# A hybrid decoder block on one core: values' evacuations and two logits tiles placed ahead of the gated branch's transposes, filler weights loaded sooner, row sums turned at a head's third step

## The chip, the cores and the metric

The kernel runs on one core of a Trainium2 chip. The metric is the device time of one execution in microseconds (us), the median of three runs. The engines are TensorE (PE, with its weight loads listed apart as PEld), VectorE (DVE), ScalarE (ACT), GpSimd (POOL) and SyncE (SP), which issues most of the DMAs. Each engine works through its own instructions in order; between engines they wait for each other's semaphores.

## The reference

One decoder block over 1024 tokens, width 1024, float32 throughout: RMSNorm, one input projection, then two branches side by side, forgetting attention and chunked spatial gating; both go into one output projection with a residual. A gated MLP with a causal convolution and a last RMSNorm follow.

```python
xn = rmsnorm(h, norm_mix_g[layer])
proj = xn @ w_in[layer]
q, k, v = ...                       # 8 heads of 64 each
log_f = jax.nn.log_sigmoid(proj[..., G_END:] + b_forget[layer])
# attention, blocks of 128 queries
logits = jnp.einsum('bqhd,bkhd->bhqk', qi, k) * scale
logits = logits + ci[..., None] - c_k          # c = cumsum(log_f)
logits = jnp.where(causal, logits, -jnp.inf)
p = jax.nn.softmax(logits, axis=-1)
att = jnp.einsum('bhqk,bkhd->bqhd', p, v)
# spatial gating, chunks of 128 tokens, 8 groups of 64
mixed = jnp.einsum('gij,bnjgd->bnigd', w, vc) + b_s.T[None, None, :, :, None]
sg = u * mixed                                 # u, vg: gelu of their part of proj
h = h + jnp.concatenate([att, sg], axis=-1) @ w_out[layer]
h = h + conv_ffn(rmsnorm(h, norm_ffn_g[layer]), ...)
return rmsnorm(h, norm_final_g)
```

## The kernel before, in words

[...]

**Stages.** Input projection (gate values u and v, then attention values, then queries and keys), spatial gating, attention, output projection with residual and second norm, up-projection with convolution, down-projection. The values' product is finished last of the first stage; its last four tiles leave PSUM through `evac_v` (L655): a ScalarE copy scaled by the row's norm, and a VectorE instruction for the remainder. Both write V. Helpers hide their line: these instructions stand under L44 in the profile.

**Spatial gating.** `spatial` (L679) does 24 matmuls (L690 to L692), and for each of eight groups two VectorE instructions that write A (again under L44), the gated branch's result, in place of u. `turn_sg(hf)` (L698) transposes one half of it in four groups of four transposes (L705), each group into one bank; ScalarE casts the bank into G (L707) and VectorE subtracts for the remainder (L708). The output projection of the gated branch needs G.

**Attention.** Eight heads. `logits(h, j)` (L778) takes query block j of head h: GpSimd masks the diagonal block (L790), TensorE does two matmuls per 512 keys (L796, L797) into a PSUM tile of 1024 columns, VectorE adds the forgetting sums, clips and takes the minimum in one instruction (L798), and ScalarE exponentiates and adds up the row sums (L800). Blocks go from 7 (1024 keys) down to 0 (128 keys). `turn_p` (L802) transposes probabilities (L813), copies them to SBUF (L814) and takes the remainder (L815); `values` (L820) multiplies them with V (L832), two halves of 512 queries per head, and `L840`/`L841` move each half's product tile to H. A head is five steps (`STEPS`); in each, the next step's `turn_p` goes out before the present step's `values`, and the next head's logits come in between, the widest tile at step 0, the one with 896 keys at step 1, two at each later step (`NEXT`). Head 0's logits have no such cover and stand ahead of the loop.

**Row sums.** `row_tail(h)` (L733), at step 1 of head h: VectorE takes the reciprocal of the row sums (L738), TensorE turns them (L739), ScalarE copies them (L740) and writes them out to DRAM (L741), and SP reads them back as a broadcast over partitions into H (L742). For the last pair of heads `pair_half` multiplies them into the products on VectorE (L756), casts (L757) and subtracts (L758); for the other pairs GpSimd does this.

**Fillers.** `sg_out` (L845) is a generator: each step is one tile of the gated branch's output projection, twelve matmuls (L874 to L876), with a residual tile loaded (L870) and the result written to DRAM (L878). `fill(key)` takes as many steps as `FILLS` (L21) says; key (-1, j) is behind head 0's logits tile j, key (h, s) behind step s of head h. The first step loads and splits its weights (`wos`).

**Loads on SP.** `head_loads(h)` issues five loads for a head's queries, keys and forgetting sums, those of heads 0 and 1 ahead of the loop. `wo_load` (L887) loads the output projection's weights near the end, which GpSimd splits (L899, L900); the loads of the up-projection's first weights (`wup`, L977 and L995) follow on SP, and L742 of the last head behind them.

**PSUM.** Eight banks of 2 KB. Attention has a pool of its own ("psb"): two tiles of 4 KB with tag "L" for logits, four of 2 KB with tag "b" for everything else, fillers too. The tags get their addresses in the order of their first use in the program. The next stage has another pool ("psc") over the same banks, with four tiles of tag "b" and four of tag "s"; a tile there waits until whatever last used its bank has been read. The output projection (`wmm`, L1026 to L1028) takes its tiles from "b" and "s" in turn, the first four with k = 0, 1, 2 ahead of k = 3.

**Order.** A scheduler places each engine's instructions by priority in program order, and by edges that hold one instruction behind another (`after`, `seq`, `Line`); `seq` keeps TensorE's attention work in the order in which it is written.

## Time and profile before

| | us |
|---|---|
| median of three runs | 1076.2 (1076.04 to 1078.09) |
| profiled execution | 1076.44 |
| its span, first to last instruction | 1074.7 |
| TensorE busy | 1054.8 |
| VectorE busy | 892.9 |
| ScalarE busy | 571.0 |
| GpSimd busy | 237.2 |

How to read it: a row of the timeline has the start in us from the span's start, the busy time, the engine, the line and operation, the tile written and those read, shapes and, behind an x, the number of instructions put together in one row; in square brackets is the engine's idle time ahead of it and what released it. A row of waits has the engine with the tile and line that waited, what it waited for, the total in us, the number of waits and the longest. "SPq" and "ACTq" are DMA issues on these engines. Attention runs from about 223 to 387 us of the span.

### The profile page before, as it was taken

What the parts mean: (1) busy time and instruction counts of PE and PEld (TensorE: products, weight loads), DVE (VectorE), ACT (ScalarE), POOL (GpSimd) and SP (SyncE); (2) the same over time, 40 slices, a digit from 0 to 9 for tenths busy, and PEclk for the clock granted to TensorE, in tenths of its full rate; (3) what the DMA queues carried; (4) which work ended last, traced back from release to release, by engine and by line L of the source; (5) the groups of instructions that cost most, each with busy time, mean ns of one, the idle gap of its engine ahead of it and who ended that gap; (6) DMA issues with size and microseconds to landing.
All of it is one profiled execution on the core that took longest, in us unless ns stands there. A gap on an engine that the chain in (4) does not pass through costs nothing.

```text
span 1074.7 us, 14461 instructions
## 1 busy us (share of the span) xinstructions
PE 1054.8 (98%) x5013; PEld 875.8 (81%) x5013; DVE 892.9 (83%) x1303; ACT 571.0 (53%) x985; POOL 237.2 (22%) x219
## 2 busy tenths in 40 slices
PE   9999999989999899999999999999999999999997
PEld 6888788778888788878888888888888888888886
DVE  5985798777777869999899999989988776898774
ACT  6666644456666845764444444444444444454653
POOL 0002134020223651054333333333322000000000
PEclk9999999999999999999999999999999999999999
DMA  9242257957556335132244523223331899433442
GB/s 338 97 140 97 68 159 213 265 165 215 162 177 225 120 128 185 72 118 97 98 137 161 172 69 127 99 98 99 107 118 46 289 327 319 123 95 97 140 125 96
DMA packets 66297, 160.80 MB, mean 150 GB/s; under 512 B 7976, under 2 KB 8240, under 8 KB 66224
## 3 DMA queue, kind: packets, MB, share of 16 engines
q1 hardware_dynamic: 65792, 159.32, 45.5%
q8 instruction: 39, 0.64, 0.2%
q10 hardware_dynamic: 432, 0.57, 0.1%
q14 instruction: 34, 0.28, 0.1%
HBM read 117.06 MB, written 42.80 MB: 149 GB/s over the span
## 4 chain that ended last, share of the span: by engine, by line
PE 74%; DVE 2%; issue 2%; DMA 2%; ACT 2%; POOL 0%; DVEq 0%; ACTq 0%; POOLq 0%; SPq 0%
PE k L1369 19%; PE qa L1117 11%; PE qc L1117 11%; PE qd L1117 11%; PE qb L1117 5%; PE pb L832 2%; PE pb L813 2%; PE pf L874 1%; PE pf L876 1%; PE pf L875 1%; PE pl L796 1%; PE pl L797 1%; DMA raw<-wos 1%; PE pb L1026 1%; PE pb L1028 1%
## 5 line engine op out<-in xcount | busy, mean ns | idle before, releaser
L1369 PE MATMUL k<-whb,wha 128*128 128x512 f32 x924 | 209.7, 389 | 0.0
L1369 PEld LDWEIGHTS k<-whb,wha 128*128 128x128 f32 x924 | 173.3, 188 | 36.2 <-DVE wha L160 0.2
L1117 PE MATMUL qc<-xT,whb 128*128 128x512 f32 x540 | 129.8, 389 | 0.0
L1117 PE MATMUL qa<-xB,wha 128*128 128x512 f32 x528 | 127.2, 390 | 0.0
L1117 PEld LDWEIGHTS qc<-xT,whb 128*128 128x128 f32 x540 | 101.3, 188 | 21.2 <-ACT whb L154 0.2
L1117 PEld LDWEIGHTS qa<-xB,wha 128*128 128x128 f32 x528 | 98.8, 188 | 20.8 <-DVE wha L160 0.4
L154 ACT CAST wha<-sg 128x512 fp32r<-128x512 f32 x77 | 47.7, 622 | 96.9 <-PE k L1369 86.6
L154 ACT CAST whb<-sg 128x512 fp32r<-128x512 f32 x82 | 50.6, 618 | 85.8 <-PE qc L1117 68.5
L160 DVE TENSOR_TENSOR wha<-sg,wha 128x512 fp32r<-128x512 f32 x77 | 52.8, 688 | 41.0 <-ACT wha L154 40.9
L1117 PE MATMUL qd<-xB,whb 128*128 128x512 f32 x264 | 63.8, 389 | 0.5 <-DVE h L1236 0.5
L1117 PE MATMUL qd<-xT,whb 128*128 128x512 f32 x264 | 63.6, 389 | 0.0
L815 DVE TENSOR_TENSOR pt<-pb,pt 128x512 fp32r<-128x512 f32 (+1 forms) x80 | 50.0, 635 | 14.5 <-ACT pt L814 13.4
L160 DVE TENSOR_TENSOR whb<-sg,whb 128x512 fp32r<-128x512 f32 x82 | 58.3, 711 | 4.4 <-ACT whb L154 4.3
L1117 PE MATMUL qb<-xT,whb 128*128 128x512 f32 x252 | 60.8, 389 | 0.0
L1004 POOL TENSOR_TENSOR sg<-raw 128x512 f32<-128x512 f32 x20 | 30.9, 1546 | 134.2 <-DVE whb L160 76.0
L1117 PEld LDWEIGHTS qd<-xB,whb 128*128 128x128 f32 x264 | 49.5, 188 | 11.2 <-issue 0.9
L1117 PEld LDWEIGHTS qd<-xT,whb 128*128 128x128 f32 x264 | 49.5, 188 | 10.3
L1117 PEld LDWEIGHTS qb<-xT,whb 128*128 128x128 f32 x252 | 47.3, 188 | 9.8
L814 ACT CAST pt<-pb 128x512 fp32r<-128x512 f32 (+1 forms) x80 | 42.5, 539 | 20.6 <-PE pb L813 14.7
L832 PE MATMUL pb<-pt,V 128*128 128x256 f32 x320 | 51.4, 285 | 1.3 <-DVE pt L815 1.2
L790 POOL TENSOR_SCALAR_AFFINE_SELECT x<-x 128x128 f32<-128x128 f32 x64 | 19.9, 312 | 129.7 <-DVE mn L798 77.4
L1007 POOL TENSOR_TENSOR sg<-sg,raw 128x512 f32<-128x512 f32 x20 | 33.3, 1664 | 64.1 <-DVE whb L160 64.1
(396 smaller groups left out, 2305.7 us busy)
## 6 DMA issues: line engine op xcount, KB each, us to landing
raw<-wup SPq DMA_DIRECT2D x44, 512.0 KB, 3.7
sg<-hx SPq DMA_DIRECT2D x77, 256.0 KB, 2.6
hx<-hs SPq DMA_DIRECT2D x44, 256.0 KB, 3.8
hx<-ca SPq DMA_DIRECT2D x35, 256.0 KB, 2.0
xT<-wdn SPq DMA_DIRECT2D x28, 256.0 KB, 4.3
raw<-wqk SPq DMA_DIRECT2D x8, 512.0 KB, 3.6
qd<-G SPq DMA_DIRECT2D x16, 256.0 KB, 3.5
kd<-G SPq DMA_DIRECT2D x16, 256.0 KB, 3.3
```

What stands on the lines that cost most here:

```text
L154: act.copy(h, src)
L160: return eng.tensor_tensor(out=l, in0=src, in1=f32(h), op=ALU.subtract)
L790: sels[h].append(pool.affine_select(out=ck[:, qs], in_=ck[:, qs], pattern=[[-1, P]], compare_op=ALU.is_ge, fill=BIG, base=0, channel_multi ...
L796: seq(pe.matmul(ps[:, c:e], A[:, qs], B[:, c:e], start=True, stop=False))
L813: seq(pe.transpose(ptr[:, c:c + P], tj[jj][:, k * P:(k + 1) * P], ident))
L814: act.copy(pt[:, 0, 0:w], ptr[:, 0:w])
L815: dve.tensor_tensor(out=pt[:, 1, 0:w], in0=ptr[:, 0:w], in1=f32(pt[:, 0, 0:w]), op=ALU.subtract)
L832: seq(pe.matmul(po[0][:, oo:oo + n], lhs, pt[:, s, o:o + n], start=(k == 0 and s == 0), stop=(s == 1 and half)))
L1004: pool.tensor_tensor(out=s[0], in0=a21, in1=a22, op=ALU.add)
L1007: pool.tensor_tensor(out=s[3], in0=s[1], in1=a12, op=ALU.add)
L1117: pe.matmul(ps, w[:, wi, ks], xb[:, xi, k, :], start=(first and n == 0), stop=(n == 11), skip_group_check=True)
L1369: pe.matmul(banks[bk + m], xh[:, xi, ms], wh[:, wi, :], start=(first and p_ == 0 and n == 0), stop=(p_ == NP - 1 and n == 2), skip_group_c ...
```

## The change

The edits, all between the end of the values and the end of attention:

- `evac_v` of the last four tiles comes ahead of `spatial()` in the program, and the Exp activation that makes ScalarE load its table is tied behind the last of them.
- `logits` is cut in two: `logits_mm` allocates the PSUM tile and issues the matmuls, `logits_end` does the rest. Head 0's blocks 7 and 6 have their matmuls ahead of `turn_sg(0)`, and their VectorE parts behind `turn_sg(0)`'s last subtraction; `turn_sg(1)` follows, and then a filler.
- Head 0's three fillers stand at 6, 4 and 2 in place of 5, 3 and 0.
- The filler stops once right behind its weights' load and split, and this part is run between `head_loads(0)` and `head_loads(1)`.
- `row_tail(h)` is called at step 2 of a head in place of step 1.

```diff
-FILLS = {(-1, j): 1 for j in (5, 3, 0)} | {(h, s): 1 for h in range(5) for s in ((0, 2, 4), (1, 3))[h % 2]}
+FILLS = {(-1, j): 1 for j in (6, 4, 2)} | {(h, s): 1 for h in range(5) for s in ((0, 2, 4), (1, 3))[h % 2]}
...
-        act.activation(v[:, tt % 2, :, 0, :], p3, AF.Copy, scale=rstd1[:, tt:tt + 1])
+        a = act.activation(v[:, tt % 2, :, 0, :], p3, AF.Copy, scale=rstd1[:, tt:tt + 1])
...
+        return a
...
-            dve.tensor_tensor(out=sgT[c][:, 1, o], in0=ps, in1=f32(sgT[c][:, 0, o]), op=ALU.subtract)
+            d = dve.tensor_tensor(out=sgT[c][:, 1, o], in0=ps, in1=f32(sgT[c][:, 0, o]), op=ALU.subtract)
+        return d
...
+    for m in range(4):
+        a = evac_v(4 + m, S[m])
+
+    after(tc, act.activation(pad[:, 0:1], eps, AF.Exp), a)
     spatial()
-    for m in range(4):
-        evac_v(4 + m, S[m])
-
-    act.activation(pad[:, 0:1], eps, AF.Exp)
     act.last = dve.last = None
...
     def logits(h, j):
+        logits_end(h, j, logits_mm(h, j))
+
+    def logits_mm(h, j):
+        A, B, B2 = abs_[h][:, 0, :], abs_[h][:, 1, :], b2s[:, h % 2, :]
+        n = (j + 1) * P
+        qs = slice(j * P, (j + 1) * P)
+        ps = psa.tile([P, 1024], F32, tag="L", bufs=2, name=nm("pl"))
+        for c in range(0, n, 512):
+            e = min(n, c + 512)
+            seq(pe.matmul(ps[:, c:e], A[:, qs], B[:, c:e], start=True, stop=False))
+            seq(pe.matmul(ps[:, c:e], A[:, qs], B2[:, c:e], start=False, stop=True))
+        return ps
+
+    def logits_end(h, j, ps, behind_=None):
...
+        m = dve.tensor_tensor_reduce(out=t, in0=ps[:, 0:n], in1=ck[:, 0:n], scale=1.0, scalar=lim[:, 0:1],
+                                     op0=ALU.add, op1=ALU.min, accum_out=mn)
+        if behind_ is not None:
+            after(tc, m, behind_)
...
         whs = split(load(0), "pool")
+        yield
...
     head_loads(0)
+    act.last = a
+    next(filler)
+    act.last = None
     head_loads(1)
-    turn_sg(0)
-    for j in range(7, -1, -1):
+    ahead_ = [(j, logits_mm(0, j)) for j in (7, 6)]
+    d = turn_sg(0)
+    for j, ps in ahead_:
+        logits_end(0, j, ps, d)
+    turn_sg(1)
+    fill((-1, 6))
+    for j in range(5, -1, -1):
         logits(0, j)
-        if j == 6:
-            turn_sg(1)
         fill((-1, j))
...
-        if s == 1:
+        if s == 2:
             if h % 2 == 0:
                 attF[h // 2] = sb("H", [P, 2, 1024])
             row_tail(h)
```

More of the change, by code (lines that the diff above doesn't have):

```diff
@@ L778, in logits @@
     def logits(h, j):
+        logits_end(h, j, logits_mm(h, j))
[10 more added lines that the diff above has]
+    def logits_end(h, j, ps, behind_=None):
         i, jj, hh = j // 2, j % 2, h % 2
-        A, B, ck, B2 = abs_[h][:, 0, :], abs_[h][:, 1, :], cks[:, hh, :], b2s[:, hh, :]
+        ck = cks[:, hh, :]
         w1, w2 = (2 * i + 1) * P, (2 * i + 2) * P
@@ L792, in logits @@
         mn = sml.tile([P, 1], F32, tag="mn", name=nm("mn"))
-        ps = psa.tile([P, 1024], F32, tag="L", bufs=2, name=nm("pl"))
-        for c in range(0, n, 512):
-            e = min(n, c + 512)
-            seq(pe.matmul(ps[:, c:e], A[:, qs], B[:, c:e], start=True, stop=False))
-            seq(pe.matmul(ps[:, c:e], A[:, qs], B2[:, c:e], start=False, stop=True))
-        dve.tensor_tensor_reduce(out=t, in0=ps[:, 0:n], in1=ck[:, 0:n], scale=1.0, scalar=lim[:, 0:1],
-                                 op0=ALU.add, op1=ALU.min, accum_out=mn)
+        m = dve.tensor_tensor_reduce(out=t, in0=ps[:, 0:n], in1=ck[:, 0:n], scale=1.0, scalar=lim[:, 0:1],
+                                     op0=ALU.add, op1=ALU.min, accum_out=mn)
+        if behind_ is not None:
+            after(tc, m, behind_)
         exs.append(act.activation(t, t, AF.Exp, bias=mn, scale=-1.0, accum_out=rows[h][:, j:j + 1]))
```

## The prediction

> **What bounds the kernel.** I read the page first, for the engine shares and the clock, and then the waits of TensorE:

> ```profile
> span 1074.7 us, 14461 instructions
> PE 1054.8 (98%) x5013; PEld 875.8 (81%) x5013; DVE 892.9 (83%) x1303; ACT 571.0 (53%) x985; POOL 237.2 (22%) x219
> PEclk9999999999999999999999999999999999999999
> ...
> PE pb L813 <- DVE pt L815: 2.9, 6, 0.7
> PE pb L739 <- DVE rs L738: 2.6, 2, 1.5
> PE pb L705 <- DVE V L44: 1.9, 1, 1.9
> ...
> PE qd L1117 <- DVE h L1236: 0.5, 1, 0.5
> ```

> TensorE is busy for 1054.8 of 1074.7 us, so no edit that only relieves another engine can gain. The change takes no matmul away; it can only close or open gaps on TensorE. The gaps near it are small: 1.9 us once ahead of the gated branch's transposes (L705) and 2.6 us at two of the eight turns of row sums (L739). If both went, without anything in their place, 4.5 us (0.4%) would be won. Behind attention TensorE waits for 0.5 us in one place (L1117), so whatever is lost by the start of the output projection is hardly made up later. The timelines of the three places follow.

> **Part 1: head 0's start.** Three edits have one answer: values evacuated before the spatial matmuls, logits tiles 7 and 6 ahead of the transposes, fillers at 6, 4, 2.

> ```profile
> 213.06 2.11 DVE L44 SCALAR_TENSOR_TENSOR V<-ps,rstd,V 128x512 fp32r<-128x512 f32 x3 [2.84 <-ACT V L44]
> 215.09 6.35 DVE L44 SCALAR_TENSOR_TENSOR A<-pb,cp,A 128x256 f32<-128x256 f32 x16
> 220.94 2.40 ACT L154 CAST whl<-raw 128x512 fp32r<-128x512 f32 x4 [5.88 <-DMA raw<-wos]
> 221.35 0.74 DVE L44 SCALAR_TENSOR_TENSOR V<-ps,rstd,V 128x512 fp32r<-128x512 f32 x1
> 221.64 5.01 POOL L160 TENSOR_TENSOR whl<-raw,whl 128x512 fp32r<-128x512 f32 x4 [3.80 <-ACT whl L154]
> 222.15 1.53 PE L705 MATMUL pb<-ident,A 128*128 128x128 f32 x12 [1.93 <-DVE V L44]
> 223.86 2.48 DVE L708 TENSOR_TENSOR G<-pb,G 128x512 fp32r<-128x512 f32 x4 [1.77 <-ACT G L707]
> 226.26 1.27 DVE L798 CUSTOM_DVE_ANT_0 t<-pl,x,lim 128x1024 f32<-128x1024 f32 x1
> 226.98 1.28 ACT L800 ACT_TABLE_LOAD   x1
> 227.46 0.69 DVE L708 TENSOR_TENSOR G<-pb,G 128x512 fp32r<-128x512 f32 x1
> 227.62 0.30 POOL L790 TENSOR_SCALAR_AFFINE_SELECT x<-x 128x128 f32<-128x128 f32 x1 [0.96 <-DVE mn L798]
> 228.40 0.40 PE L874 MATMUL pf<-whl,G 128*128 128x512 f32 x1
> 237.70 0.35 DVE L798 CUSTOM_DVE_ANT_0 gg<-pl,x,lim 128x128 f32<-128x128 f32 x1 [0.40 <-POOL x L790]
> 239.55 1.80 PE L813 MATMUL pb<-ident,t 128*128 128x128 f32 x15
> 241.55 0.74 PE L832 MATMUL pb<-pt,V 128*128 128x256 f32 x4 [0.20 <-DVE pt L815]
> ```

> Three of the four value evacuations (V) already stand ahead of the sixteen products A on VectorE; the fourth, 0.74 us behind them, is what held the transposes at 222.15. Put ahead, it doesn't vanish: the A row moves back by one V (2.11 / 3 = 0.70 us) and ends at 222.14 instead of 221.44, and the transposes of the first half need all of A. They start at 222.2, as before. What fills TensorE's gap are the eight logits matmuls (1.8 us), which need only q and k. They were due right behind those transposes, so the next transposes come 1.8 us sooner; but VectorE then sets the pace. It starts its first L708 some 0.4 us sooner (223.48 for 223.86: ScalarE's copy now stands behind nothing), and the first filler's bank is free when the fifth L708 is done. From first L708 to the end of the fifth is 223.86 to 228.15, 4.29 us, in the old order, which the new one keeps (four L708, L798 of 1024, then the fifth). That gives 227.77 and a first filler at about 227.84, against 228.40. But in the old order four logits matmuls of tile 5 were by then done; in the new one tiles 5 to 0 and all three fillers come after. Matmuls of 0.227 us (worked out below), 12 to a filler: 3 x 2.73 + 2.5 = 10.7 us, so the transposes of P (L813) start at 238.5 against 239.55. Tile 0's matmuls are now TensorE's last work ahead of them, and VectorE has to take them in (0.40 us for GpSimd's mask and 0.35 for L798, after tile 1 likewise), before the first L815 frees TensorE at L832: about 240.9 against 241.55. **Part 1 gives -0.6 us.** The bounds: -1.9 (the whole old wait of 1.93 closed and kept closed) and +0.2 (the two mask waits of 0.40 us at the end paid on top of the -0.6).

> The Exp table (1.28 us) goes from 226.98 to some 215, where ScalarE waited for the weights of the filler anyway (5.88 us idle before 220.94). Those weights are loaded two places sooner, ahead of head 1's five loads; the fillers weren't waiting for them at 228.40 (casts done at 223.34, GpSimd's differences at 226.65), and head 1's tiles are first read after 241.55, some 25 us behind the loads. On GpSimd the four differences (5.01 us) now stand ahead of the mask of tile 6, but that mask waits for L798 of tile 7 anyway (227.62). Both edits: 0, with these as cover; were the weights to land as late as before, the mask, and tile 6 behind it, would still find them split.

> **Part 2: row sums at the third step.** The old wait at head 6's turn:

> ```profile
> 364.21 1.27 DVE L798 CUSTOM_DVE_ANT_0 H<-pl,x,lim 128x1024 f32<-128x1024 f32 x1
> 365.41 0.20 DVE L738 RECIPROCAL rs<-rs 128x8 f32<-128x8 f32 x1
> 365.75 0.27 PE L739 MATMUL pb<-ident,rs 128*8 128x128 f32 x1 [1.51 <-DVE rs L738]
> 367.47 0.69 DVE L815 TENSOR_TENSOR pt<-pb,pt 128x512 fp32r<-128x512 f32 x1 [1.87 <-ACT pt L814]
> 368.32 1.15 DVE L798 CUSTOM_DVE_ANT_0 H<-pl,x,lim 128x896 f32<-128x896 f32 x1 [0.16 <-PE pl L797]
> ...
> 380.07 1.28 ACT L946 ACT_TABLE_LOAD   x1
> ```

> The reciprocal is queued on VectorE behind L798 of the next head's widest tile (1024), so TensorE, in order, waits 1.51 us. One step later the neighbour is L798 of the tile with 896 (1.15 us). In the built order of the changed kernel the reciprocal stands behind two L815 and that L798. Without the old stop TensorE gets to the small transpose at about 366.75, VectorE to the reciprocal at about 368.2: the wait of 1.5 us comes back one step later. ScalarE then has the Exp of 896 to do before the next copies of P. By the rows' durations laid end to end, L798 of tile 1 of head 7 ends 1.35 us later than before. Heads 0 to 5 show no such wait before (two in all: heads 6 and 7), since fillers or slack stood there. Head 7's turn moves behind the Sqrt table (380.07) and behind more copies. The bounds: -1.5 (the wait goes, nothing returns) and +1.35; **I take +0.7**, nearer to the upper, since the queue ahead of the reciprocal is the same by kind.

> **Part 3: a bank that the change moves without saying so.** The two logits tiles are now the first allocation in the attention's PSUM pool. Addresses go by first use: the big logits tiles ("L", two of 4 KB) were in banks 4 to 7 and are now in 0 to 3, and the four "b" tiles were in 0 to 3 and are now in 4 to 7. The output projection takes its tiles from another pool over the same banks, alternately from 0-3 and 4-7: its first at bank 0, its second at bank 4. Attention's last product tile (the "b" tile that L841 reads last) was in bank 2, which is the projection's fifth tile; it is now in bank 4, which is its second.

> ```profile
> 377.56 0.29 POOL L790 TENSOR_SCALAR_AFFINE_SELECT x<-x 128x128 f32<-128x128 f32 x1 [0.90 <-DVE mn L798]
> 377.81 1.17 POOL L899 CAST G<-raw 128x512 fp32r<-128x512 f32 x2
> 382.52 2.53 POOL L900 TENSOR_TENSOR G<-raw,G 128x512 fp32r<-128x512 f32 x2
> 381.47 3.93 SPq L995 DMA_DIRECT2D raw<-wup  x2
> 385.44 0.45 SPq L742 DMA_DIRECT2D H<-rsd  x1
> DMA to landing us min/median/max: 3.3/3.6/3.8
> 386.79 0.68 DVE L841 TENSOR_TENSOR H<-pb,H 64x512 f32<-64x512 f32 x1
> 389.23 0.39 PE L1026 MATMUL ps<-whl,A 128*128 128x512 f32 x1
> 391.69 0.69 DVE L756 TENSOR_TENSOR H<-H 128x512 f32<-128x512 f32 x1 [4.21 <-DMA H<-rsd]
> 392.41 0.69 DVE L841 TENSOR_TENSOR H<-pb,H 64x512 f32<-64x512 f32 x1
> 395.35 0.39 PE L1026 MATMUL pb<-whl,A 128*128 128x512 f32 x1
> ```

> Read from the bottom. The second L841 ends at 393.10. It needs nothing but ScalarE's copy out of the same bank, but on VectorE it stands behind L756, and L756 waits 4.21 us for the broadcast of head 7's row sums (H<-rsd). Before the change nothing on TensorE waited for it: the tile that needs this bank started at 395.35. Now the tile of 389.23 needs it. Nine matmuls (k = 0, 1, 2 of the first tile) run, and TensorE stops from 389.23 to about 393.15: **+3.9 us**. (27 matmuls lie between 389.23 and 395.35, hence 0.227 us each.) Nothing covers it, because the next tiles are queued behind on TensorE in order; the work that VectorE and ScalarE do meanwhile does not help later, where TensorE alone is the limit.

> What sets 393.1 is a chain that TensorE's earlier gains only partly move: the last mask on GpSimd (377.56, right behind L798 of tile 1), four casts and four differences of weights on GpSimd until 385.05, the second load raw<-wup on SP, which needs that buffer (issued till 385.40), then H<-rsd on SP at 385.44, landed 6.2 us later, beside the loads around it (the view of L742 gives 3.3 to 3.8 us for the others). So the stop ends later or sooner as that mask does: -0.6 (part 1) and +0.7 (part 2) move it too. The turn itself, one step later, must not pass SP's place: copied at about 383, written out some 2 us later, 385. That is just in time; if it is late by up to 1.1 us the stop grows by that.

> **The sum**: the profiled run took 1076.44 us (the span and what lies around it), 0.24 above the median of the three, 1076.2. -0.6 + 0.7 + 3.9 = +4.0, so 1080.4 in its frame, **1080.2** against the median.

> **The rivals.**
> - *The stop costs more: the clock falls* (chance 0.2). No wait of TensorE in the attention before is longer than 1.9 us, so this trace cannot show what one of 4 us does. At the start, out of idleness, eleven matmuls of 512 columns (bf16) took 4.79 us:

> ```profile
> 1.28 4.79 PE L122 MATMUL ps<-gg 128*128 128x512 bf16 x11 [1.28 <-DVE pad L133]
> ```

> That is 0.435 us each against 0.227, full speed. If the stop has this effect for about as long as it lasts, eight matmuls at 0.2 us more each are +1.6 us: 1081.8. [...]
> - *Part 2 does what it says* (0.15): -1.5 instead of +0.7, and the chain to 377.56 with it: -0.6 - 1.5 + 3.9 = +1.8, 1078.0. For it: the reciprocal's own row is 0.20 us. Against it: a wide L798 stands ahead of it in either place.
> - *The broadcast comes sooner, and the stop closes* (0.09; not slower). One mechanism: H<-rsd lands in 3.6 us, as the view has for the others, because less runs beside it. Then L756 starts at 389.0 instead of 391.7 and L841 ends at 390.45. With part 1 and the lower bound of part 2 in front of it (-2.1), TensorE resumes at 388.4, against 389.23 before: -0.8, so 1075.4. It decides from the point where L756 starts 3.9 us sooner than 391.69, all shifts together. Against it: the same loads stand beside it on SP in the new order.
> - *The bank does not bind* (0.06): a copy of L841 runs earlier than I read, and the change leaves only -0.6 + 0.7: 1076.3, or with part 2's gain 1074.1.

> **The numbers.** The forecast itself (net +4.0, part 2 anywhere in its upper half) gets 0.5, and its own range is 1079.2 to 1081.2. A difference of 0.2%, 2.15 us, is about what a measurement of this kernel can tell from no change. The forecast and the clock rival are slower by more than that; of the 0.15 of part 2 half still is: 0.78 slower. Only the last two rivals with the best of part 2 are faster by it, 0.07; the rest, 0.15, is the same. The range that holds eight in ten goes from 1077.6 (parts 1 and 2 both below what I took) to 1082.4 (the clock, or a late turn).

> **What would show it.** Right: a new line among TensorE's waits, about 4 us once, the projection's second tile (L1026's first matmul of "ps") for VectorE's H at L841; L705 gone from the list; the first L832 of head 0 about 0.6 us sooner; L739's wait still there, behind an L798 of 896; spacing of 0.43 us behind the stop only if the clock falls. Wrong: the first two projection tiles without a gap, or L739 gone with L798 of head 7's tile 1 sooner than 377; or a broadcast that lands before 389.

## The result and the profile after

The changed kernel takes 1082.65 us (median of six runs, 1081.97 to 1085.8) against 1076.3 us before (six runs), so it is 6.35 us slower by the medians; the ratio is 1.0062, 95% interval 1.0047 to 1.0076. The direction was forecast, the size was not: 1080.2 was predicted, and the measured time lies 0.25 us above the range's end of 1082.4. Of all executions in this document one is far out, 6088.91 us, one of the eleven of experiment e4; it is in no ratio.

The page of its profiled execution, then TensorE's waits (what waited, for what, total us, times, longest us). Lines have moved: L739 is now L741, L841 is L854, L1026 is L1046, L813 is L826. An operand is split into a high part (a cast) and a remainder (a subtraction), and each product is three matmuls, high by high, high by low and low by high; those of 512 columns follow each other every 0.227 us in the profile before.

```profile
span 1084.1 us, 14454 instructions
PE 1058.7 (98%) x5013; PEld 877.8 (81%) x5013; DVE 892.7 (82%) x1303; ACT 570.9 (53%) x985; POOL 236.8 (22%) x219
```

```profile
PE ps L1046 <- DVE H L854: 4.9, 1, 4.9
PE pb L826 <- DVE pt L828: 3.3, 5, 1.8
PE pb L741 <- DVE rs L740: 1.6, 1, 1.6
PE ps L258 <- DVE G L44: 1.6, 1, 1.6
PE pb L826 <- ACT t L742: 1.5, 1, 1.5
...
PE pf L888 <- DVE G L709: 1.1, 1, 1.1
...
PE pb L706 <- DVE A L44: 0.5, 1, 0.5
```

The first line is the new one: the output projection's second tile waits once for 4.9 us for VectorE's last copy out of attention's product. The 1.9 us wait at the gated branch's transposes has shrunk to 0.5 (L706), with 1.1 us new at the first filler (L888). The row sums still cost TensorE 1.6 us at head 6 and now 1.5 us at head 7, there for ScalarE's copy (L742).

This execution was the slowest of the six (1085.8). Two things in it are no steady cost of the edits, since a second profile of the same kernel has neither. The wait of 1.6 us at L258 lies at 194 us, ahead of the change, among unchanged instructions (0.8 in the profile before); and at 355.8 us TensorE waited 1.8 us for this chain, read in the timeline (start, busy us, and in brackets the idle time and its releaser):

```profile
354.40 0.29 POOL L806 TENSOR_SCALAR_AFFINE_SELECT x<-x 128x128 f32<-128x128 f32 x1 [3.38 <-DMA x<-ncd]
...
356.23 1.02 DVE L809 CUSTOM_DVE_ANT_0 t<-pl,x,lim 128x768 f32<-128x768 f32 x1 [2.45 <-POOL x L806]
...
357.87 0.52 PE L826 MATMUL pb<-ident,gg 128*128 128x128 f32 x3 [1.82 <-DVE pt L828]
```

A mask on GpSimd stood behind the load of head 7's forgetting sums, which was late in this run. (It was late in e7's profile too, with a wait of 2.1 us; what makes it late was not tested.) So the second profile, of 1082.58 us and close to the median, is the one to set against the profile before (1076.44). Its timeline, the start, the chain and the stop:

```profile
222.15 4.48 PE L706 MATMUL pb<-ident,A 128*128 128x128 f32 x32 [0.47 <-DVE A L44]
227.78 0.51 PE L888 MATMUL pf<-whl,G 128*128 128x512 f32 x1 [1.15 <-DVE G L709]
238.67 1.82 PE L826 MATMUL pb<-ident,t 128*128 128x128 f32 x15
240.97 0.75 PE L845 MATMUL pb<-pt,V 128*128 128x256 f32 x4 [0.47 <-DVE pt L828]
...
377.02 0.29 POOL L806 TENSOR_SCALAR_AFFINE_SELECT x<-x 128x128 f32<-128x128 f32 x1 [0.63 <-DVE mn L809]
384.97 0.45 SPq L744 DMA_DIRECT2D H<-rsd  x1
387.93 0.39 PE L1048 MATMUL pb<-G,G 128*128 128x512 f32 x1
391.43 0.69 DVE L758 TENSOR_TENSOR H<-H 128x512 f32<-128x512 f32 x1 [5.00 <-DMA H<-rsd]
392.15 0.68 DVE L854 TENSOR_TENSOR H<-pb,H 64x512 f32<-64x512 f32 x1
392.89 0.79 PE L1046 MATMUL ps<-whl,A 128*128 128x512 f32 x1 [4.57 <-DVE H L854]
393.48 0.63 PE L1047 MATMUL ps<-whl,A 128*128 128x512 f32 x1
...
397.32 0.63 PE L1047 MATMUL pb<-whl,A 128*128 128x512 f32 x1
397.74 0.44 PE L1048 MATMUL pb<-whl,A 128*128 128x512 f32 x1
398.02 0.40 PE L1046 MATMUL pb<-whl,A 128*128 128x512 f32 x1
```

The account against before: at head 0's first product (L845) TensorE is 0.58 us ahead (240.97 for 241.55). The last mask is 0.54 us ahead (377.02 for 377.56). The projection's second tile starts at 392.89 in place of 389.23: +3.66. (TensorE itself comes to the projection 1.05 us sooner than before, at 386.03 for 387.08, which is why its wait there reads 4.57 us.) From 392.89 to 398.02 twelve matmuls take 5.13 us where 12 x 0.227 = 2.72 would do: +2.4. Together +6.1, and the two executions differ by 6.14. The windows view of this stretch shows the clock that these matmuls ran at (the third number from the end is the granted clock, 0.50 in the middle row):

```profile
390.00:392.00 2.00, 0.00 (x0) 0.00 (x0) 0.57 (x1) 0.00 (x0) 0.00 (x0) 0.75 1.01 363
...
394.00:396.00 2.00, 2.00 (x6) 1.55 (x5) 1.32 (x3) 1.81 (x4) 0.00 (x0) 0.50 0.16 64
396.00:398.00 2.00, 2.00 (x6) 1.55 (x5) 2.00 (x3) 0.89 (x2) 1.71 (x2) 0.54 0.00 0
```

### The profile page after: what moved, and what is told of

Same layout as the page of the kernel before. It is cut to its first block, busy times and chain, and to the rows that moved or that the text cites. A ratio compares the mean times of both kernels' runs of the same rounds, so it can differ in the third digit from the quotient of the medians.

```text
span 1084.1 us, 14454 instructions
## 1 busy us (share of the span) xinstructions
PE 1058.7 (98%) x5013; PEld 877.8 (81%) x5013; DVE 892.7 (82%) x1303; ACT 570.9 (53%) x985; POOL 236.8 (22%) x219
## 4 chain that ended last, share of the span: by engine, by line
PE 68%; issue 6%; DVE 4%; ACT 2%; DMA 2%; POOL 2%; POOLq 0%; SPq 0%; DVEq 0%; ACTq 0%
PE k L1389 19%; PE qa L1137 11%; PE qc L1137 11%; PE qd L1137 11%; PE qb L1137 5%; PE ps L258 2%; PE pb L826 1%; PE pb L1046 1%; PE pb L1047 1%; PE pb L1048 1%; PE pb L845 1%; DMA x<-ncd 1%; DVE G L44 1%; PE ps L1082 1%; DMA H<-rsd 1%
## 5 line engine op out<-in xcount | busy, mean ns | idle before, releaser
L154 ACT CAST wha<-sg 128x512 fp32r<-128x512 f32 x77 | 47.8, 622 | 96.8 <-PE k L1389 85.4
L154 ACT CAST whb<-sg 128x512 fp32r<-128x512 f32 x82 | 50.5, 618 | 85.1 <-PE qc L1137 68.0
L160 DVE TENSOR_TENSOR wha<-sg,wha 128x512 fp32r<-128x512 f32 x77 | 52.8, 687 | 39.9 <-ACT wha L154 39.7
L160 DVE TENSOR_TENSOR whb<-sg,whb 128x512 fp32r<-128x512 f32 x82 | 58.2, 710 | 4.4 <-ACT whb L154 4.3
L845 PE MATMUL pb<-pt,V 128*128 128x256 f32 x320 | 52.0, 287 | 0.5 <-DVE pt L828 0.5
```

The costliest lines, as they stand in the source:

```text
L154: act.copy(h, src)
L160: return eng.tensor_tensor(out=l, in0=src, in1=f32(h), op=ALU.subtract)
L845: seq(pe.matmul(po[0][:, oo:oo + n], lhs, pt[:, s, o:o + n], start=(k == 0 and s == 0), stop=(s == 1 and half)))
```

## The experiments

Two theories were set against each other: *bank* (attention's last product tile shares its PSUM bank with the projection's second tile; the stop and the clock behind it are the whole loss) and *turns* (the row sums at the third step delay heads 6 and 7). Which bank that last tile falls into was read from each built program; the ratios are to runs of the kernel before made beside them (medians of 1076.4 to 1076.8). Line numbers in the rows of e3 to e11 are those of each kernel and shift by a few:

| kernel | its bank | needed by the projection's | median us | ratio to before (95%) |
|---|---|---|---|---|
| before | 2 | fifth tile | 1076.3 | |
| changed | 4 | second | 1082.65 | 1.0062 (1.0047 to 1.0076) |
| e1 changed, again | 4 | second | 1083.6 | 1.0059 (1.0045 to 1.0073) |
| e2 other banks | 4 | fifth | 1075.23 | 0.9987 (0.9978 to 0.9996) |
| e3 collision alone | 4 | second | 1083.2 | 1.0056 (1.0042 to 1.0069) |
| e4 turn third alone | 1 | seventh | 1076.59 | 0.9997 (0.9988 to 1.0006) |
| e5 kept busy | 4 | second | 1081.87 | 1.0049 (1.0036 to 1.0062) |
| e6 sums first | 4 | second | 1076.6 | 1.0001 (0.9993 to 1.0010) |
| e7 copy first | 4 | second | 1077.19 | 1.0001 (0.9992 to 1.0010) |
| e8 last turn second | 5 | eighth | 1075.99 | 0.9996 (0.9987 to 1.0006) |
| e9 allocation back | 0 | first | 1087.47 | 1.0105 (1.0090 to 1.0119) |
| e10 turn second | 5 | eighth | 1075.67 | 0.9992 (0.9983 to 1.0001) |
| e11 start only | 1 | seventh | 1078.8 | 1.0018 (1.0010 to 1.0027) |

**e1, the changed kernel again.**

> The changed kernel once more, for a second profile. Bank theory: median near 1082.6, +6 on the kernel before; one wait of TensorE for VectorE's H at the output projection's second tile, 4 to 5 us, and seven matmuls spaced 0.43 us behind it. The 2.0 us wait at 355.8 us in the first profile (behind GpSimd's mask, behind the load of head 7's forgetting sums) is not part of the change and should be smaller here. Rival (turns of row sums): the same time, but the added waits lie inside heads 6 and 7 and not in the projection.

The stop is there (4.57 us), the wait at 355.8 us is not, and eleven matmuls, not seven, are 0.43 us apart, at a granted clock of 0.50. The added time lies where the bank theory has it, at the projection, and not in heads 6 and 7.

**e2, other banks.** Only the assignment of the projection's first eight tiles to banks differs.

```diff
-    banks8 = {(tt, hf): (bank() if hf == 0 else sbank()) for tt in first for hf in range(2)}
+    b8 = [(bank() if hf == 0 else sbank()) for tt in first for hf in range(2)]
+    banks8 = {(tt, hf): b8[[0, 2, 4, 6, 1, 3, 5, 7][2 * n + hf]] for n, tt in enumerate(first) for hf in range(2)}
```

> The changed kernel, with the output projection's first four tiles all in banks 0 to 3 and the next four in 4 to 7, so that bank 4 is needed by the fifth tile. Nothing else differs. Bank theory: the stop at the second tile and the half clock behind it go, 5.5 to 6.5 us less than the changed kernel: 1076 to 1077.2. Rival (turns): within 1 us of the changed kernel, since heads 6 and 7 still carry the loss.

Some 7 us less, even a little below before. The timeline of its profile, the second tile and VectorE's second copy:

```profile
387.48 0.39 PE L1046 MATMUL pb<-whl,A 128*128 128x512 f32 x1
...
390.39 0.68 DVE L854 TENSOR_TENSOR H<-pb,H 64x512 f32<-64x512 f32 x1
```

The copy is still late, 2.9 us behind the start of the second tile, and TensorE doesn't care: the tile lies elsewhere. It beats the kernel before by 0.13%, less than the 0.2% taken at the outset as what can be told from no change.

**e3, the collision alone.** The kernel before, with these two edits:

```diff
+    firstl.append(psa.tile([P, 1024], F32, tag="L", bufs=2, name=nm("pl")))
     turn_sg(0)
...
-        ps = psa.tile([P, 1024], F32, tag="L", bufs=2, name=nm("pl"))
+        ps = firstl.pop() if firstl else psa.tile([P, 1024], F32, tag="L", bufs=2, name=nm("pl"))
...
-        if s == 1:
+        if s == (2 if h == 1 else 1):
```

> The kernel before, with two edits that only move PSUM addresses: a logits tile is allocated first, and head 1's row sums alone turn at the third step (head 1 had no wait there). Attention's last product tile then lies in bank 4, as in the changed kernel; heads 6 and 7 and the start are as before. Bank theory: a stop of 3.9 us at the projection's second tile and about 1.6 us of half clock: +5 to +6, 1081.5 to 1082. Rival (turns, or the start): within 1 us of before.

Neither the start nor heads 6 and 7 are changed, and the whole loss is there: 6.4 us, above what was expected. In its profile:

```profile
393.89 0.79 PE L1028 MATMUL ps<-whl,A 128*128 128x512 f32 x1 [3.41 <-DVE H L842]
394.48 0.63 PE L1029 MATMUL ps<-whl,A 128*128 128x512 f32 x1
```

Behind a wait of 3.4 us came slow matmuls, eight of them here (393.89 to 397.38), at a granted clock of 0.50 (394 to 396 us). The turns of heads 6 and 7 are not the cause.

**e4, the row sums at the third step alone** (the kernel before with `if s == 2`).

> The kernel before, with all row sums turned at the third step and nothing else; the last product tile comes to lie in bank 1, the projection's seventh tile, so no stop there. Bank theory: the term alone, +0.7 (between -1.5 and +1.35): 1076.5 to 1077.7. Rival (turns): +4 to +6, 1080 or more.

The time is that of before (-0.03%). Of the profile's waits those at the turns and one at the projection, then VectorE's rows around head 6's turn:

```profile
PE pb L739 <- DVE rs L738: 1.6, 1, 1.6
PE pb L813 <- ACT t L740: 1.5, 1, 1.5
...
PE pb L1026 <- DVE H L841: 0.4, 1, 0.4
```

```profile
366.08 1.14 DVE L798 CUSTOM_DVE_ANT_0 H<-pl,x,lim 128x896 f32<-128x896 f32 x1
367.14 0.08 DVE L798 DVE_READ_ACCUMULATOR2_ANT mn<- 128x1 f32 x1
367.14 0.20 DVE L738 RECIPROCAL rs<-rs 128x8 f32<-128x8 f32 x1
```

The wait did come back behind the L798 of 896, as forecast. But TensorE, without its stop a step earlier, had fed VectorE sooner: that L798 starts at 366.08 instead of 368.32. What the new wait costs was won before it. The last of the three waits is a small collision of e4's own: in the built program the product tile before the last lies in bank 0, that of the projection's first tile. From attention's first product to the projection's first matmul TensorE takes 145.62 us here and 145.53 before, so without these 0.4 us the later turn would win about 0.3.

**e5, TensorE kept busy.** The changed kernel with eighteen matmuls whose result is overwritten:

```diff
+            if (tt, hf) == (0, 1):
+                for sp_ in ((4, 0), (1, 0)):
+                    for n in range(9):
+                        pe.matmul(banks8[sp_], attT[0][:, 0, 0:P], wo[0][0][:, 0, :], start=True, stop=True)
             wmm(tt, hf, banks8[tt, hf], (0, 1, 2))
```

> The changed kernel with 18 spare matmuls (4.1 us) of no use in front of the projection's second tile, into banks that are overwritten later, so that TensorE works through most of the 4.6 us stop; the bank comes free no sooner. Clock theory: the matmuls behind keep the 0.227 us spacing, and the 2.4 us that eleven of them cost in the second profile of the changed kernel are won: 1080 to 1081. Rival (the slow matmuls come from something else, such as traffic of the loads): the spacing of 0.43 us stays and the time is 1082.5 to 1084.

```profile
388.52 4.25 PE L1111 MATMUL pb<-whl,A 128*128 128x512 f32 x18
393.32 0.50 PE L1046 MATMUL ps<-whl,A 128*128 128x512 f32 x1 [0.55 <-DVE H L854]
393.65 0.40 PE L1047 MATMUL ps<-whl,A 128*128 128x512 f32 x1
...
421.15 1.06 PE L1082 MATMUL ps<-ident,xn 128*128 128x128 f32 x8 [0.81 <-DVE xn L1064]
```

With work in the stop there is no slow matmul behind it: from 393.65 to 397.78 they are 0.23 us apart (0.43 in e1), and the mean granted clock of the execution is 0.998, as before the change, against 0.995 in e1. The loads are the same in both programs, so in this pair the fall of the clock went with the idle time and not with the loads. But the median is only 1.7 us under e1's, and 0.8 under the changed kernel's first runs, where 2.4 was expected, and the intervals of the ratios overlap: the time alone does not show the gain. The rows say where part of it goes. The second tile starts 0.43 us later than in e1 (393.32 for 392.89), and TensorE, faster now, reaches the transposes of the normalised rows (L1082) ahead of VectorE and waits 0.8 us, where e1, slower by then, does not wait.

**e6, the broadcast ahead of the loads.** Two issues of `wup` on SP are held behind head 7's L744.

```diff
+        if i < AHEAD:
+            after(tc, d, rowd[7])
```

> The changed kernel, with the broadcast of head 7's row sums (L744) issued on SP ahead of the two second loads of wup rather than behind them. Chain theory (GpSimd's weights, the load that needs their buffer, then the broadcast): the broadcast is issued at about 384 as soon as the row sums are written, lands with less beside it by 388, and the stop shrinks from 4.6 us to under 1 us with no half clock behind it: 1076 to 1077.5. Rival (the turn of row sums itself is late, SP's place does not matter): stop of 3.5 us or more, 1081 to 1083.

```profile
385.07 0.45 SPq L745 DMA_DIRECT2D H<-rsd  x1
385.62 1.56 SPq L1016 DMA_DIRECT2D raw<-wup  x2
```

```profile
388.90 0.69 DVE L759 TENSOR_TENSOR H<-H 128x512 f32<-128x512 f32 x1 [0.19 <-DMA H<-rsd]
389.62 0.68 DVE L855 TENSOR_TENSOR H<-pb,H 64x512 f32<-64x512 f32 x1
```

Issued at 385.07 with the loads behind it, the broadcast is used from 388.90, 3.8 us later (6.5 in e1). The bank is free at 390.3, about when TensorE comes to it, and the loss is gone although the banks are as in the changed kernel.

**e7, VectorE's copy first.** The multiplication by the row sums (L758) is held behind the second L854.

> The changed kernel, with VectorE's copy out of attention's last product tile (the second L854) held ahead of the multiplication that waits for the broadcast (L758); banks, turns and SP's order unchanged. Bank theory: the bank is free at 387.5, before TensorE gets to it at 388.2: no stop, 1074.5 to 1076.5, as with other banks. Rival (TensorE waits for the broadcast in another way): a stop of 3 us or more stays, 1081 or more.

VectorE's second copy and TensorE's second tile:

```profile
390.15 0.69 DVE L856 TENSOR_TENSOR H<-pb,H 64x512 f32<-64x512 f32 x1 [0.42 <-ACT H L855]
```

```profile
391.48 0.39 PE L1049 MATMUL ps<-whl,A 128*128 128x512 f32 x1
```

The copy is done at 390.84 and TensorE does not stop at the projection; the multiplication behind it still waits for the broadcast, until 394.48. The median, 1077.19, is 0.7 us above what was expected, within the spread of its runs (1075.33 to 1078.75). It was VectorE's order, not the broadcast as such, that held the bank.

**e8, head 7's turn back to the second step** (with e2's banks).

> The changed kernel with the projection's banks as in the run with other banks, and head 7's row sums turned at the second step again, the others at the third. With the third step TensorE waits 1.5 us at head 7 for ScalarE's copy of the row sums behind a table load; with the second step it waited 1.1 us for the reciprocal. If these waits are on the path: 0.3 to 0.8 us less than with other banks alone, 1074.4 to 1075.2; if the broadcast or something behind it sets the end: no difference.

No gain over e2: TensorE loses 1.3 us for the reciprocal in place of 1.5 us for ScalarE's copy.

**e9 and e10, one half of the bank shift undone each; e11, both.** e9 takes the first small tile ahead of the logits tiles (`firstb.append(bank())`, used by `turn_sg(0)`); e10 turns the row sums at the second step; e11 does both.

> The changed kernel with the attention pool's first allocation put back (a small tile before the first logits tile, so big tiles in banks 4 to 7 and small ones in 0 to 3 as before); the row sums stay at the third step. With that, attention's last product tile falls into bank 0, the bank of the projection's first tile. Bank theory: the stop does not go, it comes one tile sooner, at L1046's first matmul, from about 386.1 to 392.8: +5.7 on the kernel before, and half clock behind it, +1.2 to +2.4: 1083.3 to 1084.8. Rival (the address order of big and small tiles is what matters, by itself): 1075 to 1077.

> The changed kernel with all row sums turned at the second step as before; the big tiles stay in banks 0 to 3. The last product tile falls into bank 5, the projection's eighth tile. Bank theory: no stop, 1075 to 1077, although the turn's own term is small. Rival (allocation order alone): the stop stays, 1082 or more.

> The changed kernel with both put back, allocation and turn, so that the edits at head 0's start are left alone; the last product tile falls into bank 1, the projection's seventh. Theory: the start's term alone, -0.4 to -0.8: 1075.4 to 1076.2. Rival (the start gains more than the profile's 0.6 us at head 0, since the run with other banks was 1.3 us under the one with the turns alone): 1074.5 to 1075.2.

e9: worse than the change itself, by more than was expected. TensorE stops ahead of the very first tile:

```profile
393.45 0.69 DVE L759 TENSOR_TENSOR H<-H 128x512 f32<-128x512 f32 x1 [5.34 <-DMA H<-rsd]
...
395.00 0.76 PE L1048 MATMUL pb<-whl,A 128*128 128x512 f32 x1 [7.13 <-DVE H L855]
```

e10: no stop. Its median is 0.9 us under before, but the interval of the ratio (0.9983 to 1.0001) does not rule out that it is the same. So both edits together make the collision: the allocation order decides in which half the small tiles lie, and the step at which the row sums take their tile decides which of the four is last. e11 was a miss, 1078.8 where 1075.4 to 1076.2 was expected, and its profile names the reason:

```profile
215.21 6.35 DVE L44 SCALAR_TENSOR_TENSOR A<-pb,cp,A 128x256 f32<-128x256 f32 x16
...
221.66 0.47 PE L791 MATMUL pl<-x 128*128 128x512 f32 x1 [2.15 <-issue]
```

With the big tiles back in banks 4 to 7, the first logits tile falls onto banks that hold the spatial products, and waits until VectorE has read the last of them (215.21 + 6.35 = 221.56). The row names no releaser ("issue"); the built program has the first logits tile in banks 4 and 5 and the last spatial product in bank 4. It is the same kind of collision at the other end of attention; e9 pays it too (2.1 us). The order of allocation that the change brought in helps the start (e10 has no such wait) and, with the later turn, hurts the end.

## Why the prediction was right or wrong

- **What bounds the kernel**: right that TensorE alone decides; VectorE's and ScalarE's busy time hardly moved. But "it can only close or open gaps on TensorE" left something out: of the 6.1 us only 3.7 come from gaps, and 2.4 are TensorE's own matmuls at half clock (0.50 granted).
- **Part 1, -0.6**: right in its size and its steps. First filler at 227.78 (forecast 227.84), L826 at 238.67 (238.5), first product at 240.97 (about 240.9). Of the 0.58 us, 0.11 lay ahead of the changed stretch already (the first spatial matmul at 214.06 for 214.17), so some 0.5 belongs to the edits. The times cannot tell so little: e10, which has this part alone with free banks, has a ratio of 0.9992 (0.9983 to 1.0001). Costing the weights' earlier load and the Exp table at nothing held as well, as far as no wait for them appears.
- **Part 2, +0.7**: the mechanism was right, its size wrong. The step that failed in this part is "VectorE [gets] to the reciprocal at about 368.2": it was 367.14 in e4, since the L798 in front of it started 2.2 us sooner than in the old timeline, not at its old place. L798 of tile 1 ends where it did (377.40 in e4, 377.49 before); by the time the term is 0 (e4: -0.03%, interval -0.12 to +0.06%), and by the profile a few tenths to the good: from attention's first product to the projection's first matmul e1 takes 145.06 us, against 145.53 before and 145.93 in e10, which keeps the old turn.
- **Part 3, +3.9**: right in place, cause and chain. Its own size, taken out of the shifts in front of it, is 3.66 + 0.54 = 4.2 in the second profile: the broadcast took 0.2 us more, and the rest is VectorE and TensorE's handover. It named the allocation order alone as what moved the bank; e9 and e10 show that the turn's step is the other half.
- **The step that failed**: behind the stop the sum went on at full clock, "TensorE stops from 389.23 to about 393.15: +3.9 us. Nothing covers it", and the falling clock was a rival with a chance of 0.2, the author's estimate: in attention the trace before has no wait above 1.9 us, so it did not show what one of 3.9 does. The clock fell to 0.50 in every profile with this stop, at waits of 3.4, 4.6, 4.9 and 7.1 us. The rival's price, "eight matmuls at 0.2 us more each are +1.6", was of the right size: the four profiles lost 1.7, 2.4, 1.5 and 1.8 us, in this order. That the second profile of the changed kernel lost 2.4, in twelve long intervals, is the upper end. With the terms as measured there, -0.6 + 0 + 4.2 + 2.4 = +6.0. With 1.5, the price in the first profile of the same kernel, the sum would be +5.1: how far the time lies from the forecast is in part chance, that the clock cost something is not.
- **The broadcast rival** had the right lever: in e6 the broadcast is used 3.8 us after its issue, and the loss is gone. In the changed kernel the loads beside it were unchanged, as was held against it.

## What to carry to other kernels

Where pools of two stages share PSUM banks, the order of allocation is part of the schedule: before a reordering is costed, list which bank each stage's last-read tile and the next stage's first tiles get in both programs. An edit that looks like one on the row sums can move a tile to a bank where someone waits, and the cheapest remedy may be to give the next stage's tiles out in another order (e2: 1075.23 us for 1082.65). And a TensorE stop of the length seen here, 3.4 us and more, should be priced with the clock that it loses, 1.5 to 2.4 us in these profiles.

## What the runs showed of the hardware

```profile
396.00:398.00 2.00, 1.03 (x3) 0.84 (x4) 1.94 (x4) 0.62 (x1) 0.00 (x0) 0.64 0.99 399
398.00:400.00 2.00, 2.00 (x6) 1.61 (x5) 1.32 (x3) 1.73 (x4) 0.00 (x0) 0.51 0.22 90
```

What it cost here is about half of the low stretch that lies behind the wait: half of 392.9 to 397.8 is 2.5 us in e1, where the rows gave 2.4, and half of 397.0 to 400.0 is 1.5 in the first profile after, as in its rows. The longest stop, 7.1 us in e9, cost 1.8.

**The clock fell once after a shorter wait.** In the first profile after, TensorE waited 1.8 us up to 357.9 us, and from 359 us the windows show a granted clock of 0.50, for 3.4 us (it is 0.79 from 362 to 363):

```profile
358.00:359.00 1.00, 1.00 (x9) 0.96 (x9) 1.00 (x2) 0.85 (x4) 0.88 (x1) 1.00 0.22 57
359.00:360.00 1.00, 1.00 (x6) 0.91 (x5) 1.00 (x5) 1.00 (x3) 0.80 (x2) 0.50 0.06 20
361.00:362.00 1.00, 1.00 (x6) 1.00 (x5) 0.97 (x2) 0.08 (x1) 1.00 (x2) 0.50 0.63 197
```

In e7 a wait of 2.1 us at the same place left the granted clock at 1.00 (all windows from 352 to 364 us). In the first profile after, the half clock set in 1.1 us behind the wait's end; that this wait caused it is not shown. The number of slow matmuls behind the stop at the projection went from seven to eleven between two executions of one program. So the price has a spread of almost 1 us from run to run, and this may be part of why the changed kernel's runs spread over 3.8 us; that was not tested.
